# The tail of a row-skewness kernel: one partial sum moved from VectorE to ScalarE, VectorE's last two steps made one

## Chip, cores and metric

One core of one Trainium2 chip. The metric is device time in microseconds (us) of one execution; a number for a kernel is the median of its runs. Engine names are those of the profile: PE (TensorE matmul), PEld (TensorE weight load), DVE (VectorE), ACT (ScalarE), POOL (GpSimd), SP (SyncE). A trailing q (DVEq, ACTq, SPq) is the engine's sequencer, which handles waits and issues.

## What is computed

```python
rows, cols = 1024, 8192          # x: float32
mean = np.mean(x, axis=-1, keepdims=True)
std = np.std(x, axis=-1, keepdims=True)
z = (x - mean) / (std + 1e-8)
return np.mean(z ** 3, axis=-1)
```

The kernel computes it from raw moments. With m1, m2, m3 the row means of x, x² and x³, and var = m2 − m1², the skewness is (m3 − 3·m1·(m2 − (2/3)·m1²)) · var^(−1.5).

## The kernel before

**Blocks.** The 1024 rows are 8 blocks of 128 rows (row p·8+b is partition p of block b). A block is loaded in units (`UNITS`, line 19): two of 4096 columns in the first four blocks, and ever smaller ones behind that, the last block in eight units of 1152, 1152, 1152, 896, 1024, 1152, 896 and 768 columns. All loads are issued on SP's queue (line 206) into eight rotating buffers. The order of work on each engine is the order in the source (a manual schedule); waits between instructions are added by the framework.

**Per slice.** ScalarE squares a slice of x and accumulates its sum into one column of `s2u` (line 213, an ACTIVATE and an accumulator read). VectorE multiplies the square by x and accumulates into one column of `s3u` (line 218, a SCALAR_TENSOR_TENSOR and an accumulator read). TensorE transposes x in chunks of 128 columns and adds the transposes up in PSUM (line 231). In the last block one slice is one unit, so its eight slices fill eight columns of `s2u` and `s3u`; the square of the very last slice goes to PSUM (`sqps`) and not to SBUF.

**Statistics.** The blocks 0 to 6 are finished while the last block is worked on (lines 146 to 197). The tail of the last block (lines 241 to 263) is what the change touches:

- ScalarE copies the transposed sums out of PSUM (line 127) and sums the eight columns of `s2u` into `m2` and the first six of `s3u` into `m3` (line 247). The last two columns of `s3u`, those of the last but one slice (`j - 2`) and of the last one (`j - 1`), are not ready yet.
- TensorE turns the copy into the row means `m1` (line 130).
- ScalarE makes `m1sq` = m1² (line 253), `nm1` = −3·m1 (line 254), `v3` = m2 − (2/3)·m1sq (line 255) and `t` = nm1·v3 + m3 (line 256).
- GpSimd makes `var` = m2 − m1sq (line 257) and `rr` = var^(−1.5) (line 258).
- VectorE, behind its last slice (`cube`, line 218), makes `num` = s3u[j−2] + t + s3u[j−1] (line 259), then `skew` = num·rr (line 263).
- SP waits for the last eight loads (lines 265 to 267) and for VectorE's last step, and writes the result out (line 268).

The profile shortens names: `m_l` may be `m2` or `m3` of the tail, `v_l` is `v3`, `nm_l` is `nm1`.

**Waits.** In the built program a compute instruction holds one semaphore wait itself; further ones go to a wait instruction on the same engine's sequencer just ahead of it (the DVEq, ACTq rows of the trace). `num` has a sequencer wait for VectorE's own last accumulator read and holds a wait for `t` itself. `skew` has a sequencer wait for `num` and holds a wait for `rr` itself. `v3` holds a wait for `m1sq`, and `t` one for `v3`, both of their own engine.

Of the kernel before, what the change touches and what calls it, by code (L numbers as in the profile page):

```python
# [9 lines left out]
AF = mybir.ActivationFunctionType  # L10
ALU = mybir.AluOpType
# [48 lines left out]
def kernel(  # L60
# [11 lines left out]
    NB = R // P  # L72
    L = NB - 1
# [22 lines left out]
    def small(name, n):  # L96
        return onep.tile([P, n], FP, tag=name, name=name)
# [9 lines left out]
    s2u, s3u = sums[:, 0 : NB * K], sums[:, NB * K :]  # L107
# [5 lines left out]
    skew = small("skew", NB)  # L113
# [4 lines left out]
    act, g, v = nc.scalar.activation, nc.gpsimd, nc.vector  # L118
# [10 lines left out]
    def mean(b):  # L129
        nc.tensor.matmul(  # L130
            out=s1ps[:, b : b + 1], lhsT=Tsb[b % 2], rhs=onesn, start=True, stop=True
        )
# [23 lines left out]
    def first_rest():  # L156
# [8 lines left out]
        out=m1a[:, 0:nw], in0=s1ps[:, 0:nw], in1=s1a, op=ALU.add))  # L165
# [23 lines left out]
    def third_2():  # L189
# [7 lines left out]
        out=skew[:, F : F + 1], in0=mid["t"], in1=mid["rr"], op=ALU.mult))  # L197

    for b, widths in enumerate(UNITS):
        tp = tps[b] = psum.tile([P, P], FP, tag="tp", name=f"tp_{b}")  # L200
        c0 = 0
        j = b * K
        for k, (w, n_slices) in enumerate(widths):
# [4 lines left out]
            for s, e in _slices(w, n_slices):  # L208
                if last_unit:
                    sq = psum1.tile([P, e - s], FP, tag="sqps", name="sqps")  # L210
                else:
                    sq = sqpool.tile([P, e - s], FP, tag="sq", name=f"sq_{b}_{k}_{s}")
                act(  # L213
                    out=sq, in_=xt[:, s:e], func=AF.Square, scale=s_scale,
# [4 lines left out]
                    out=cube, in0=sq, scalar=1.0, in1=xt[:, s:e],  # L219
                    op0=ALU.mult, op1=ALU.mult, accum_out=s3u[:, j : j + 1],  # L220
# [3 lines left out]
            if w_act:  # L224
                act(  # L225
                    out=same[:, 0:w_act], in_=xt[:, w - w_act : w], func=AF.Copy,
                    scale=inv_n, accum_out=s1a[:, b : b + 1],
                )
            n = (w - w_act) // P
            for c in range(n):  # L230
                nc.tensor.matmul(  # L231
                    out=tp, lhsT=xt[:, c * P : (c + 1) * P], rhs=ident,
# [6 lines left out]


    n, m1 = n_sl[L], s1ps[:, L : L + 1]
    m2, m3, m1sq, nm1, var, v3, rr, t, num = (
        small(f"{t}_l", 1) for t in ("m2", "m3", "m1sq", "nm1", "var", "v3", "rr", "t", "num")
    )

    def row_sum(out, src, n):
        act(out=junk[:, 0:n], in_=src[:, L * K : L * K + n], func=AF.Copy, accum_out=out)

    copy_sums(L)
    row_sum(m2, s2u, n)  # L250
    row_sum(m3, s3u, n - 2)
    mean(L)
    act(out=m1sq, in_=m1, func=AF.Square)
    act(out=nm1, in_=m1, func=AF.Copy, scale=-3.0)
    act(out=v3, in_=m1sq, func=AF.Identity, scale=-2.0 / 3.0, bias=m2)
    act(out=t, in_=v3, func=AF.Identity, scale=nm1, bias=m3)
    g.tensor_tensor(out=var, in0=m2, in1=m1sq, op=ALU.subtract)
    g.tensor_tensor(out=rr, in0=var, in1=expo[:, 0:1], op=ALU.pow)
    v.scalar_tensor_tensor(  # L259
        out=num, in0=s3u[:, j - 2 : j - 1], scalar=t, in1=s3u[:, j - 1 : j],  # L260
        op0=ALU.add, op1=ALU.add,
    )
    v.tensor_tensor(out=skew[:, L:NB], in0=num, in1=rr, op=ALU.mult)  # L263

    seen = nc.sync.nop()
    for ld in loads[-8:]:
# [32 lines left out]
```

## Time and profile before

| | |
|---|---|
| median of 5 runs | 90.92 us (90.86 to 91.01) |
| the profiled execution: time | 90.89 us |
| its span, first to last instruction | 89.1 us |
| time outside of the span | 1.79 us |
| granted TensorE clock, mean | 0.97 |
| DVE, ACT busy | 74.1 us (83%), 74.2 us (83%) |
| VectorE's last slice ends | 86.25 us into the span |
| the last compute step (`skew`) ends | 86.85 us into the span |
| write of the result: issue, issue to landing | at 86.88 us, 1.4 us |

The time is the whole execution, the span what lies between its first and last instruction. A timeline row reads: start in us from the span's beginning, length in us, engine, source line, operation, output<-inputs, shape; what stands in square brackets is how long the engine was idle and what released it. "issue" in the chain of work is time in which an engine waited for nothing that the profile shows.

### The profile page before, as it was taken

The page shows a single profiled execution, that of the slowest core. Times are in us where ns is not written, and L with a number is a line of the kernel's source. Part 1 is how long each engine was busy: PE and PEld are TensorE (multiplying, and loading weights), DVE is VectorE, ACT ScalarE, POOL GpSimd, SP SyncE. Part 2 cuts the span into 40 slices and gives each one's busy share as a digit, 9 for nine tenths or more (in the row PEclk, how much of TensorE's full clock was granted, in tenths as well). Part 3 has the DMA queues.
Part 4 walks back from the last instruction along what each step waited for, and adds up shares of the span by engine and source line. Part 5 has one row for each costly group of instructions (what it writes and reads, how often), then busy time and mean ns, then how long its engine had stood idle before and what let it go on. Part 6 is the DMA issues. An engine that isn't in the chain of part 4 may idle for free.

```text
span 89.1 us, 1436 instructions
## 1 busy us (share of the span) xinstructions
PE 63.5 (71%) x504; PEld 58.2 (65%) x504; DVE 74.1 (83%) x111; ACT 74.2 (83%) x136; POOL 13.7 (15%) x18
## 2 busy tenths in 40 slices
PE   0002999583492935999998899488997989888910
PEld 0002989482491925999997799378896868677710
DVE  1000399999799498999999999999999999999980
ACT  6002999789992999999799999599999999999960
POOL 3000000000000000000000000000000089999830
PEclk9999999999999999569999999999999999999995
DMA  4899999999999999999999999999999999997000
GB/s 118 324 419 441 434 419 441 434 419 441 434 419 427 427 427 427 434 419 433 408 436 394 413 436 422 430 419 419 419 403 430 405 412 414 407 409 273 17 0 2
DMA packets 4038, 33.64 MB, mean 378 GB/s; under 512 B 576, under 2 KB 576, under 8 KB 2368
## 3 DMA queue, kind: packets, MB, share of 16 engines
q1 hardware_dynamic: 4032, 33.56, 90.5%
q8 instruction: 4, 0.07, 0.3%
q14 instruction: 2, 0.02, 0.0%
HBM read 33.55 MB, written 0.00 MB: 377 GB/s over the span
## 4 chain that ended last, share of the span: by engine, by line
DMA 55%; DVE 22%; issue 10%; ACT 5%; SPq 4%; DVEq 0%; ACTq 0%
DMA x<-in_x_dram 55%; DVE sq L218 21%; ACT sq L213 5%; SPq L206 4%; DVE cube L218 1%; DVE num_l L259 0%; DVE skew L263 0%; DVE m23m L176 0%; DVEq L218 0%; DVEq L263 0%; DVEq L259 0%; ACTq L213 0%
## 5 line engine op out<-in xcount | busy, mean ns | idle before, releaser
L218 DVE SCALAR_TENSOR_TENSOR sq<-sq,x 128x1568 f32<-128x1568 f32 (+20 forms) x51 | 72.3, 1477 | 11.7 <-ACT sq L213 11.5
L213 ACT ACTIVATE sq<-x 128x1568 f32<-128x1568 f32 (+20 forms) x51 | 63.9, 1256 | 11.2 <-DMA x<-in_x_dram 10.7
L231 PE MATMUL tp<-ident,x 128*128 128x128 f32 x488 | 61.5, 285 | 14.4 <-DMA x<-in_x_dram 14.2
L231 PEld LDWEIGHTS tp<-ident,x 128*128 128x128 f32 x488 | 56.8, 148 | 17.9 <-DMA x<-in_x_dram 9.2
L153 POOL TENSOR_TENSOR vara<-m23a,m1sqa 128x6 f32<-128x6 f32 x1 | 2.0, 1987 | 70.4 <-ACT m1sq3a L157 70.4
L213 ACT ACTIVATION_READ_ACCUMULATOR sq<-x 128x1 f32 x51 | 9.5, 186 | 0.0
L130 PEld LDWEIGHTS s1ps<-onesn,tsb 128*128 128x128 f32 x16 | 2.4, 188 | 9.1 <-ACT tsb L127 9.1
L130 PE MATMUL s1ps<-onesn,tsb 128*128 128x1 f32 x16 | 3.0, 254 | 7.4 <-ACT tsb L127 7.4
L218 DVE DVE_READ_ACCUMULATOR sq<-sq,x 128x1 f32 x51 | 4.2, 82 | 0.0
L225 ACT ACTIVATE same<-x 128x1024 f32<-128x1024 f32 x3 | 3.1, 1041 | 0.0
L154 POOL TENSOR_TENSOR rra<-vara,expo 128x6 f32<-128x6 f32 x1 | 2.9, 2877 | 0.1
L127 ACT COPY tsb<-tp 128x128 f32<-128x128 f32 x8 | 1.9, 244 | 0.0
L102 ACT ACT_TABLE_LOAD x1 | 1.3, 1283 | 0.7 <-PEq L283 0.7
L184 POOL TENSOR_TENSOR rr<-var,expo 128x1 f32<-128x1 f32 x1 | 1.4, 1427 | 0.1
L161 POOL TENSOR_TENSOR m23a<-m23a,m1sq3a 128x6 f32<-128x6 f32 x1 | 1.3, 1268 | 0.1
L160 POOL TENSOR_TENSOR m1sq3a<-m1sq3a,nm1a 128x6 f32<-128x6 f32 x1 | 1.2, 1202 | 0.1
L162 POOL TENSOR_TENSOR skew<-m23a,rra 128x6 f32<-128x6 f32 x1 | 1.2, 1201 | 0.1
L183 POOL TENSOR_TENSOR var<-m23m,m1sq 128x1 f32<-128x1 f32 x1 | 1.0, 1043 | 0.0
L218 DVE SCALAR_TENSOR_TENSOR cube<-sqps,x 128x768 f32<-128x768 f32 x1 | 1.0, 955 | 0.0
L196 POOL TENSOR_TENSOR skew<-t,rr 128x1 f32<-128x1 f32 x1 | 0.8, 842 | 0.1
L213 ACT ACTIVATE sqps<-x 128x768 f32<-128x768 f32 x1 | 0.8, 796 | 0.0
L100 DVE MEMSET onesn<- 128x1 f32 x1 | 0.1, 59 | 0.8 <-PEq L283 0.8
(34 smaller groups left out, 7.8 us busy)
## 6 DMA issues: line engine op xcount, KB each, us to landing
x<-in_x_dram SPq DMA_DIRECT2D x8, 2048.0 KB, 23.6
x<-in_x_dram SPq DMA_DIRECT2D x2, 1472.0 KB, 30.0
x<-in_x_dram SPq DMA_DIRECT2D x3, 832.0 KB, 18.0
x<-in_x_dram SPq DMA_DIRECT2D x4, 576.0 KB, 10.7
x<-in_x_dram SPq DMA_DIRECT2D x2, 896.0 KB, 22.9
x<-in_x_dram SPq DMA_DIRECT2D x1, 1728.0 KB, 32.8
x<-in_x_dram SPq DMA_DIRECT2D x1, 1408.0 KB, 25.3
x<-in_x_dram SPq DMA_DIRECT2D x1, 1216.0 KB, 23.4
```

Of the source, the lines that this page charges most:

```text
L102: nc.scalar.activation(out=tiny, in_=onesn, func=AF.Square)
L127: nc.scalar.copy(out=Tsb[b % 2], in_=tps[b])
L130: nc.tensor.matmul(out=s1ps[:, b : b + 1], lhsT=Tsb[b % 2], rhs=onesn, start=True, stop=True)
L153: g.tensor_tensor(out=vara, in0=m2a, in1=m1sqa, op=ALU.subtract)
L154: g.tensor_tensor(out=rra, in0=vara, in1=expo, op=ALU.pow)
L161: g.tensor_tensor(out=m3a, in0=m3a, in1=m1sq3a, op=ALU.add)
L184: g.tensor_tensor(out=mid["rr"], in0=mid["var"], in1=expo[:, 0:1], op=ALU.pow)
L206: loads.append(nc.sync.dma_start(out=xt, in_=xv[b, :, c0 : c0 + w]))
L213: act(out=sq, in_=xt[:, s:e], func=AF.Square, scale=s_scale, accum_out=s2u[:, j : j + 1],)
L218: v.scalar_tensor_tensor(out=cube, in0=sq, scalar=1.0, in1=xt[:, s:e], op0=ALU.mult, op1=ALU.mult, accum_out=s3u[:, j : j + 1],)
L225: act(out=same[:, 0:w_act], in_=xt[:, w - w_act : w], func=AF.Copy, scale=inv_n, accum_out=s1a[:, b : b + 1],)
L231: nc.tensor.matmul(out=tp, lhsT=xt[:, c * P : (c + 1) * P], rhs=ident, start=(k == 0 and c == 0), stop=(c0 == C and c == n - 1), is_transp ...
```

## The change

ScalarE's sum of the first six columns of `s3u` goes to a tile of its own, `m3p`. A new ScalarE instruction, between `nm1` and `v3`, adds the column of the last but one slice to it: `m3` = s3u[j−2] + m3p. `t` now holds seven of the eight columns, and VectorE's two closing steps become one: skew = (s3u[j−1] + t)·rr. The tile `num` goes.

```diff
-    m2, m3, m1sq, nm1, var, v3, rr, t, num = (
-        small(f"{t}_l", 1) for t in ("m2", "m3", "m1sq", "nm1", "var", "v3", "rr", "t", "num")
+    m2, m3p, m3, m1sq, nm1, var, v3, rr, t = (
+        small(f"{t}_l", 1) for t in ("m2", "m3p", "m3", "m1sq", "nm1", "var", "v3", "rr", "t")
     )
...
     copy_sums(L)
     row_sum(m2, s2u, n)
-    row_sum(m3, s3u, n - 2)
+    row_sum(m3p, s3u, n - 2)
     mean(L)
     act(out=m1sq, in_=m1, func=AF.Square)
     act(out=nm1, in_=m1, func=AF.Copy, scale=-3.0)
+    act(out=m3, in_=s3u[:, j - 2 : j - 1], func=AF.Identity, bias=m3p)
     act(out=v3, in_=m1sq, func=AF.Identity, scale=-2.0 / 3.0, bias=m2)
     act(out=t, in_=v3, func=AF.Identity, scale=nm1, bias=m3)
     g.tensor_tensor(out=var, in0=m2, in1=m1sq, op=ALU.subtract)
     g.tensor_tensor(out=rr, in0=var, in1=expo[:, 0:1], op=ALU.pow)
     v.scalar_tensor_tensor(
-        out=num, in0=s3u[:, j - 2 : j - 1], scalar=t, in1=s3u[:, j - 1 : j],
-        op0=ALU.add, op1=ALU.add,
+        out=skew[:, L:NB], in0=s3u[:, j - 1 : j], scalar=t, in1=rr,
+        op0=ALU.add, op1=ALU.mult,
     )
-    v.tensor_tensor(out=skew[:, L:NB], in0=num, in1=rr, op=ALU.mult)
```

In the built program the new ScalarE instruction has a sequencer wait for VectorE's accumulator read of the last but one slice, and holds a wait for `m3p`. VectorE's closing step has one sequencer wait for two things, its own last accumulator read and `t`, and holds a wait for `rr`. On PE nothing differs. On GpSimd the same instructions stand in the same order with the same waits. SP issues the same transfers in the same order; the write of the result waits for VectorE's closing step as before.

## The prediction

> **What bounds the kernel now.** I read the page's first part and its chain of work first, then the chain in order of time from 84 us on, then the timelines of ScalarE and GpSimd over the same stretch. On the page:
>
> ```profile
> span 89.1 us, 1436 instructions
> ...
> DMA 55%; DVE 22%; issue 10%; ACT 5%; SPq 4%; DVEq 0%; ACTq 0%
> ```
>
> The chain is loading for over half of the span and VectorE's slices after that. The change touches nothing of either: its first edited instruction runs after 85 us, so only the last 1.5 us before the write can move. That stretch of the chain (start us, length us, what):
>
> ```profile
> 84.27 1.10 DVE sq L218 x3
> 85.37 0.89 DVE cube L218 x2
> 86.26 0.03 issue
> 86.29 0.02 DVEq L259
> 86.31 0.06 issue
> 86.37 0.23 DVE num_l L259
> 86.60 0.03 issue
> 86.62 0.02 DVEq L263
> 86.64 0.04 issue
> 86.69 0.16 DVE skew L263
> ```
>
> VectorE's last slice with its accumulator read ends at 86.26. Then 0.11 us go by for a sequencer wait and the start (0.03 + 0.02 + 0.06), num takes 0.23, another 0.09 go by in the same way, and skew takes 0.16 to 86.85. SP issues the write at 86.88. All behind that (the write's 1.4 us and the program's end) waits for this one instant, so the time moves one for one with the end of VectorE's closing step: 86.85 before.
>
> What ScalarE does meanwhile, from its timeline; the first three rows are the same operation in the block before, with the instructions around it:
>
> ```profile
> 79.90 0.18 ACT L213 ACTIVATION_READ_ACCUMULATOR sq<-x 128x1 f32 x1
> 79.99 0.28 ACT L187 ACTIVATE v<-m1sq,m23m 128x1 f32<-128x1 f32 x1
> 80.20 1.06 ACT L213 ACTIVATE sq<-x 128x1024 f32<-128x1024 f32 x1
> ...
> 85.34 0.17 ACT L253 ACTIVATE m1sq_l<-s1ps 128x1 f32<-128x1 f32 x1
> 85.41 0.17 ACT L254 ACTIVATE nm_l<-s1ps 128x1 f32<-128x1 f32 x1
> 85.54 0.29 ACT L255 ACTIVATE v_l<-m1sq_l,m_l 128x1 f32<-128x1 f32 x1
> 85.87 0.39 ACT L256 ACTIVATE t_l<-v_l,m_l,nm_l 128x1 f32<-128x1 f32 x1
> ```
>
> t ends at 86.26, in the same instant as VectorE's last slice: the two arms are level, with nothing to spare that could be counted on. Two rules of ScalarE are to be read here. Instructions with no wait on each other overlap: nm_l starts 0.07 after m1sq_l starts. Instructions that wait on each other don't: v_l starts 0.03 after m1sq_l ends (85.51), t_l 0.04 after v_l ends (85.83). The third arm is GpSimd's:
>
> ```profile
> 85.59 0.19 POOL L257 TENSOR_TENSOR var_l<-m_l,m1sq_l 128x1 f32<-128x1 f32 x1 [1.19 <-ACT nm_l L254]
> 85.86 0.54 POOL L258 TENSOR_TENSOR rr_l<-var_l,expo 128x1 f32<-128x1 f32 x1
> ```
>
> rr ends at 86.40 by this rough record. Before, only skew at 86.69 needed it; now the closing step does, at once.
>
> **What goes from VectorE.** Before, 86.26 to 86.85 is 0.11 + 0.23 + 0.09 + 0.16 = 0.59 us. After, one wait and one step: 0.11 and 0.22 (the duration of num, 218 ns, which has the same operation, shape and a pointer scalar as the new step). With all its inputs ready the closing step would run 86.37 to 86.59, 0.26 us earlier. That is the most that the change can give: 90.92 − 0.26 = **90.66 us**.
>
> **What comes to ScalarE.** The new m3 is an ACTIVATE with one pointer operand (its bias) on 128x1, as L187 is; that row gives 0.28 us, and the next instruction on ScalarE started 0.21 after it (79.99 to 80.20), its wait over by then or not, so 0.21 is what m3 holds the engine for at the most in that row. Its start: nm_l ends at 85.58, and back-to-back rows overlap by about 0.09 (79.90 + 0.18 against 79.99), so the engine has room from 85.49. m3 adds a wait, for VectorE's accumulator read of the last but one slice, which ends at 85.37; with the 0.11 of a sequencer wait and start that is 85.48, level with the engine's own 85.49. So this wait costs about nothing, and if VectorE is later in some execution its own last slice is later by the same, before and after. Queued behind m3 are v3 and t, and for t waits VectorE's closing step. I take m3 from 85.50.
>
> - v3 starts at 85.50 + 0.21 = 85.71 instead of 85.54 (m1sq has long ended) and ends 0.29 later at 86.00.
> - t starts 0.04 after that, at 86.04, and ends 0.39 later at 86.43 instead of 86.26.
> - The sequencer wait on VectorE, now for its own slice and for t together, ends with t: 86.43 + 0.11 = 86.54. Closing step to 86.54 + 0.22 = **86.76**.
>
> m2, m1sq and nm1 stand ahead of m3, so GpSimd's var and rr start as before. SP's queue is moved past nothing, and its transfers are the same.
>
> **What rr may cost.** No row of before shows VectorE held up by GpSimd. From below: rr ends at 86.40, and an engine holding its wait itself starts 0.04 after the release in the rows of ScalarE to VectorE (accumulator read 30.23 + 0.18, VectorE from 30.45): 86.44, earlier than 86.54, so nothing. From above: skew, which held the same wait, ran at 86.69, so rr was there by then, and the closing step would end at 86.69 + 0.22 = 86.91. I take the lower end, since the record of rr's end is the nearest row and it would have to be off by 0.10 to count.
>
> **Sum.** 86.76 − 86.85 = −0.09 us. Against the profiled execution that is 90.89 − 0.09 = 90.80; that execution lies 0.03 below the median of the runs, so for a median I forecast 90.92 − 0.09 = **90.83 us**. Of 0.26 us that leave VectorE, 0.17 come back as a later t.
>
> **A rule of the skill against it.** The trace has VectorE's plain add at 0.16 us (skew, TENSOR_TENSOR) and its add with a pointer at 0.22, and ScalarE's at 0.28. The Trainium skill, "ScalarE: Activation LUTs", section "Rules for kernel authors", would keep an add on VectorE. By that rule alone, with each add priced as a lone instruction, the move would lose 0.28 − 0.16 = 0.12 us. The rows agree on the prices, but the rule is about work per element, and here each step on VectorE also has 0.09 to 0.11 of wait and start. The same page, section "What ACT_TABLE_LOAD costs", gives an overlap of about 93 ns between back-to-back ACTIVATEs and about 280 ns for one with a pointer bias; by those, as an estimate, m3 would hold the engine 0.19 us and t would end 0.02 earlier.
>
> **Rivals.** About 0.2% (0.18 us) is what a measurement of this kernel can tell from no change, so the lines are at 90.74 and 91.10.
>
> 1. *ScalarE hides most of m3.* m1sq and nm1 start 0.07 apart. If m3 too gives its place up after 0.07, t ends at 86.33, the closing step starts at 86.44 (where rr also lets it) and ends at 86.66: −0.19, **90.73 us**, with 90.66 as the floor. For it: ScalarE idles in v3's wait for m1sq before (85.49 to 85.54), and the 0.21 behind L187 may hold some of the next load's wait. Against: those two take immediate operands and last 0.17; L187 with a pointer lasts 0.28.
> 2. *rr becomes the bound.* GpSimd's records are rough. If rr is seen only between 86.54 and 86.69, the time lies between 90.83 and 90.92 + 0.06 = **90.98 us**. For it: nothing before shows that rr was early. Against: two records, 0.19 and 0.54 long, would have to be short by some tenth.
> 3. *ScalarE doesn't overlap at m3, and the change loses.* If m3 with its sequencer wait starts only when nm1 has ended, and v3 only when m3 has ended, m3 runs from 85.58 + 0.11 = 85.69 to 85.97, v3 from 86.01 to 86.30, t from 86.34 to 86.73, and the closing step from 86.84 to 87.06: +0.21, **91.13 us**. Without the 0.11 at m3's start (0.03 in its place) it is 0.08 less, 91.05. The place is the ScalarE stretch from nm1 to t. It decides from the point where t comes over 0.26 us later than before (86.52); beyond 86.70 the loss is over 0.2%. For it: t has two fresh inputs and v3 and t are already strictly serial. Against: v3 doesn't use m3, and L187, which also has a sequencer wait, started 0.09 before the instruction ahead of it ended.
>
> That the change does not do what it says is excluded by the built order: one instruction less on VectorE, one more on ScalarE, in the places given.
>
> **Chances and range.** Forecast 0.60, rival 1 0.20, rival 2 0.10, rival 3 0.10. Faster by over 0.2%: rival 1 with 0.20, and 0.05 of the forecast, whose 0.09 a scatter such as that of the five runs (0.15 between the ends) can carry over the line: 0.25. Slower by over 0.2%: 0.08 of rival 3. Within: 0.55 + 0.10 + 0.02 = 0.67. The range goes from the floor, 90.66, to rival 3 with the short start, 91.05, which takes in both ends of rr; only rival 3's far end, under 1 in 10, is left out.
>
> **What would show it.** In the changed profile: an ACTIVATE m3 at about 85.50, 0.28 long; v3 about 0.21 after its start; t ending at 86.43, clearly behind VectorE's last slice at 86.26; one closing step of 0.22, started 0.11 after t's end; the distance from the end of VectorE's last slice to the end of the closing step 0.50 instead of 0.59. If v3 starts 0.07 behind m3, it is rival 1; if the step starts well over 0.11 after t, it is rival 2; if v3 starts only after m3's end, rival 3. A change anywhere ahead of 85 us would make the working wrong as a whole.

## The result and the profile after

| | before | after |
|---|---|---|
| median | 90.96 us (90.83 to 91.30, 47 runs) | 90.84 us (90.66 to 91.04, 26 runs) |
| ratio after / before | | 0.9984, 95% interval 0.9978 to 0.9991 |
| profiled execution: time, span | 90.89, 89.1 us | 90.72, 88.9 us |
| end of VectorE's last accumulator read | 86.25 us | 86.23 us |
| end of the closing step | 86.85 us | 86.67 us |
| **tail**: from the one to the other | 0.60 us | 0.44 us |

The ratio is a gain of 0.15 us (0.08 to 0.20), under the 0.2% line of the prediction. The first column holds 47 runs where the table ahead of the prediction has 5, and its median is 0.04 us higher. All comparisons below are ratios to runs of before on the same chip. Where they are too coarse, the tail is read from a kernel's one profile; two further profiles show how far to trust it: late_before has the tail of before (0.60) and late_after that of after (0.44), each within 0.01 us. The expectations give after's tail as 0.43; by the rows it is 86.67 − 86.23 = 0.44.

The page after counts one compute instruction less on VectorE (110 for 111) and one more on ScalarE (137 for 136); the one by which the total falls is a wait of SP behind the write. The chain no longer ends on VectorE's slices but runs through ScalarE:

```profile
span 88.9 us, 1435 instructions
...
DMA 62%; ACT 23%; issue 5%; SPq 4%; DVE 2%; ACTq 0%; DVEq 0%
```

The larger share of ACT does not come from more work there (74.4 us busy, 74.2 before): VectorE and ScalarE run side by side for most of the span, and the chain, followed back from the end, now passes along ScalarE. Its last pieces in order of time (start us, length us, what):

```profile
85.40 0.05 issue
85.45 0.29 ACT m_l L255
85.74 0.19 ACT v_l L256
85.94 0.02 issue
85.96 0.40 ACT t_l L257
86.36 0.04 DVEq L260
86.39 0.06 issue
86.45 0.22 DVE skew L260
```

VectorE's sequencer wait ends with t at 86.36 + 0.04, and the closing step starts 0.06 later: by this chain t decides. The timeline of the same stretch after, ScalarE and GpSimd, then VectorE's last two rows:

```profile
85.32 0.17 ACT L253 ACTIVATE m1sq_l<-s1ps 128x1 f32<-128x1 f32 x1
85.39 0.17 ACT L254 ACTIVATE nm_l<-s1ps 128x1 f32<-128x1 f32 x1
85.45 0.29 ACT L255 ACTIVATE m_l<-sums,m3p_l 128x1 f32<-128x1 f32 x1
85.56 0.19 POOL L258 TENSOR_TENSOR var_l<-m_l,m1sq_l 128x1 f32<-128x1 f32 x1 [1.18 <-ACT nm_l L254]
85.65 0.28 ACT L256 ACTIVATE v_l<-m1sq_l,m_l 128x1 f32<-128x1 f32 x1
85.83 0.54 POOL L259 TENSOR_TENSOR rr_l<-var_l,expo 128x1 f32<-128x1 f32 x1
85.96 0.39 ACT L257 ACTIVATE t_l<-v_l,m_l,nm_l 128x1 f32<-128x1 f32 x1
86.15 0.08 DVE L218 DVE_READ_ACCUMULATOR cube<-sqps,x 128x1 f32 x1
86.45 0.22 DVE L260 SCALAR_TENSOR_TENSOR skew<-sums,t_l,rr_l 128x1 f32<-128x1 f32 x1 [0.22 <-POOL rr_l L259]
```

m3 (`m_l`, L255) starts 0.06 behind nm1, v3 starts 0.20 behind m3 while m3 is still running (to 85.74), and t ends at 86.35. Before, t ended 0.01 behind VectorE's slice; now it ends 0.12 behind it. So the added instruction made t 0.11 later, not 0.17. rr ends at 86.37, as far behind VectorE's slice (0.14) as before within 0.02. Which of the two, t or rr, the closing step waits for can't be told from ends that lie 0.02 apart: the chain goes through t, the last row names rr. That is what the first experiments are for. Theory A is that t decides and that m3 made it late; theory B is that rr decides and t has slack.

### The profile page after: what moved, and what is told of

The parts are those of the page before. It is cut to its first block, busy times and chain, and to the rows that moved or that the text cites. A ratio compares the mean times of both kernels' runs of the same rounds, so it can differ in the third digit from the quotient of the medians.

```text
span 88.9 us, 1435 instructions
## 1 busy us (share of the span) xinstructions
PE 63.5 (71%) x504; PEld 58.3 (66%) x504; DVE 73.9 (83%) x110; ACT 74.4 (84%) x137; POOL 13.6 (15%) x18
## 4 chain that ended last, share of the span: by engine, by line
DMA 62%; ACT 23%; issue 5%; SPq 4%; DVE 2%; ACTq 0%; DVEq 0%
DMA x<-in_x_dram 62%; ACT sq L213 19%; SPq L206 4%; DVE sq L218 2%; ACT sqps L213 1%; ACT junk L247 1%; ACT t_l L257 0%; ACT m_l L255 0%; ACT t L190 0%; DVE skew L260 0%; ACT v_l L256 0%; ACT v L187 0%; ACT tsb L127 0%; ACT m1sq3a L157 0%; ACT nm1a L158 0%
```

## The experiments

All tails are from the end of VectorE's last accumulator read to the end of the closing step.

### 1. The added half alone: two_steps

Edit of the changed kernel:

```diff
-        out=skew[:, L:NB], in0=s3u[:, j - 1 : j], scalar=t, in1=rr,
-        op0=ALU.add, op1=ALU.mult,
+        out=num, in0=s3u[:, j - 1 : j], scalar=t, in1=sums[:, K - 1 : K],
+        op0=ALU.add, op1=ALU.add,
     )
+    v.tensor_tensor(out=skew[:, L:NB], in0=num, in1=rr, op=ALU.mult)
```

> The added half of the change alone: ScalarE adds the last but one column (m3), and VectorE still ends with two steps with a wait between them, num = s3u[j-1] + t + a column of zeros, then skew = num x rr. The result is the same. Tail = time from the end of VectorE's last accumulator read to the end of the closing step, 0.60 us before and 0.43 us after the change. Theory A (t is the arm that decides after the change, m3 made it 0.11 later against VectorE's last slice): num starts 0.10 behind t's end, tail = 0.22 + 0.22 + 0.10 + 0.16 = 0.70, so slower than before by 0.10 us (ratio 1.001). Theory B (GpSimd's rr decides after the change, t has slack): rr is only needed by skew, which is late anyway, num starts behind VectorE's own slice as before, tail 0.60, the time of before.

Measured: ratio 0.9999 (0.9990 to 1.0009), the time of before. In the profile VectorE's last read ends at 86.24, and t ends as late behind it as in the changed kernel (0.12); the chain's last pieces:

```profile
85.97 0.40 ACT t_l L257
86.36 0.02 issue
86.39 0.23 DVE num_l L261
...
86.71 0.16 DVE skew L265
```

The tail is 0.63. The chain runs through t, as theory A has it, but num starts only 0.03 behind t, not 0.10. Here num holds the wait for t itself, and the sequencer wait ahead of it (for VectorE's own slice) is over by then. Where the late one sits in the sequencer wait, as in the changed kernel, it costs 0.10. So the added instruction alone costs 0.03 in the tail and not 0.10: a miss in size that came from the price of the wait. The times are too coarse to show 0.03.

### 2. The fused step alone: no_m3

Edit of the changed kernel:

```diff
-    act(out=m3, in_=s3u[:, j - 2 : j - 1], func=AF.Identity, bias=m3p)
...
-    act(out=t, in_=v3, func=AF.Identity, scale=nm1, bias=m3)
+    act(out=t, in_=v3, func=AF.Identity, scale=nm1, bias=m3p)
```

> The fused closing step alone: ScalarE does not add the last but one column, which is left out of the sum altogether. So ScalarE's tail is that of before, VectorE's that of after. Theory A (t decides after the change): t ends level with VectorE's slice again, the closing step starts at whichever comes later, 0.11 behind the slice or some 0.04 to 0.08 behind rr (0.14 behind the slice in the changed profile): tail 0.33 to 0.44; by A alone 0.36, some 0.24 us faster than before, 0.07 faster than after. Theory B (rr decides, 0.08 behind its end): tail stays 0.43 to 0.44, as after, 0.17 us faster than before.

Measured: ratio 0.9966 (0.9954 to 0.9978), 0.31 us faster than before (0.20 to 0.42), with after's interval not reaching that ratio. The profiled execution is the slowest of the twelve (90.98; their median is 90.71). In it VectorE ran 0.23 us later than in before's profile, and it did so long before the edited lines (the slice at 78.51 us stood 0.23 later too), while ScalarE stood as in it (m1sq starts at 85.33, 85.34 before), so t (86.26) and rr (86.39) were ready before VectorE's last slice ended. Its chain is VectorE's alone:

```profile
85.59 0.89 DVE cube L218 x2
86.48 0.03 issue
86.51 0.05 DVEq L259
86.56 0.06 issue
86.62 0.22 DVE skew L259
```

The tail is 0.37: VectorE's last read ends at 86.47, and 0.15 later, behind the waits and the start (0.03 + 0.05 + 0.06 in the chain), the step of 0.22 begins. The sequencer wait for two things took 0.05 and not the 0.02 of before. That is the floor of the fused step, 0.23 under before's 0.60. So the removal is worth up to 0.23, and the changed kernel keeps 0.16 of it: 0.07 of its tail come from t. The times say more than the tail here (0.31 against 0.23); the interval takes 0.23 in, and what the rest is stays open. That profile can't tell what rr would do with VectorE on time; run 6 gives the price for it. It also shows VectorE elsewhere against ScalarE than the other profiles have it, which run 8 takes up.

### 3. The power taken out of the closing step: no_rr

Edit of the changed kernel:

```diff
-        out=skew[:, L:NB], in0=s3u[:, j - 1 : j], scalar=t, in1=rr,
+        out=skew[:, L:NB], in0=s3u[:, j - 1 : j], scalar=t, in1=mid["rr"],
```

> The changed kernel, but its closing step multiplies by the power of the block before (long ready), so it does not wait for the last block's rr, which is still computed; the last block's power is left out of the result. The number and places of the waits are the same. Theory A (t decides): tail 0.43, the time of after. Theory B (rr decides): the tail is shorter than 0.43, by as much as rr is later than t; as both ended within 0.02 us in the changed profile, by 0.02 to 0.05 at the most, since the wait for t comes next.

Measured: tail 0.44 (VectorE's last read ends at 86.18; t ends at 86.30):

```profile
85.91 0.39 ACT L257 ACTIVATE t_l<-v_l,m_l,nm_l 128x1 f32<-128x1 f32 x1
...
86.40 0.22 DVE L260 SCALAR_TENSOR_TENSOR skew<-sums,t_l,rr 128x1 f32<-128x1 f32 x1 [0.22 <-POOL rr_l L259]
86.77 0.35 SPq L268 DMA_DIRECT2D out_dram<-skew  x1
```

The step starts 0.10 behind t, as in after, though it doesn't read the last block's rr: theory A. The releaser that the row names, rr_l, isn't read by this step at all: releasers are inferred, and between two ends so close the inference picked the wrong one. The time, ratio 0.9989 (0.9978 to 1.0000), is not to be set against after: the third row shows the write issued 0.15 behind the closing step where after has 0.03 (86.70 behind 86.67). The instructions in the trace explain it: the write now holds a wait for GpSimd itself, and the wait for VectorE moved into a wait instruction on SP's sequencer, with a second one behind it.

### 4. The disputed instruction twice: m3_twice

Edit of the changed kernel:

```diff
     act(out=m3, in_=s3u[:, j - 2 : j - 1], func=AF.Identity, bias=m3p)
+    act(out=spare, in_=sums[:, K - 1 : K], func=AF.Identity, bias=m3p)
```

> The changed kernel with a second such ACTIVATE (128x1, pointer bias, on a column of zeros, result unused) right behind m3 and ahead of v3. Doubles the cost in dispute. Theory A with m3 priced by its place in the queue (0.20 us from its start to v3's): v3 starts 0.40 behind m3's start, t ends 0.20 later, tail 0.63 to 0.64, 0.20 us slower than after and 0.03 slower than before. If ScalarE hid most of such an instruction (a place of 0.07): tail 0.50. If each held the engine for its whole length (0.28): tail 0.71. Theory B (rr decides, t has slack): less than 0.20 by that slack, which the changed profile puts under 0.02.

Measured: ratio 0.9999 (0.9987 to 1.0012), 0.14 us over after's ratio, though the intervals overlap at their ends (after's reaches 0.9991). The profile is sharper; ScalarE's rows:

```profile
85.39 0.29 ACT L255 ACTIVATE m_l<-sums,m3p_l 128x1 f32<-128x1 f32 x1
85.59 0.28 ACT L257 ACTIVATE spare_l<-sums,m3p_l 128x1 f32<-128x1 f32 x1
85.77 0.28 ACT L258 ACTIVATE v_l<-m1sq_l,m_l 128x1 f32<-128x1 f32 x1
86.08 0.39 ACT L259 ACTIVATE t_l<-v_l,m_l,nm_l 128x1 f32<-128x1 f32 x1
```

Starts lie 0.20 and 0.18 apart: that is the place such an instruction takes. t ends 0.31 behind VectorE's last read (86.16), where after has 0.12, and the tail is 0.63, 0.19 more. That is theory A with its price, to 0.01 us. ScalarE neither hides it (a place of 0.07) nor runs it strictly alone (0.28).

### 5. Is it the new wait? m3_no_wait, and the order: m3_behind_v3

m3_no_wait, edit of the changed kernel:

```diff
-    row_sum(m3p, s3u, n - 2)
+    row_sum(m3p, s3u, n - 3)
...
-    act(out=m3, in_=s3u[:, j - 2 : j - 1], func=AF.Identity, bias=m3p)
+    act(out=m3, in_=s3u[:, j - 3 : j - 2], func=AF.Identity, bias=m3p)
```

> The changed kernel, but m3 adds the column ahead of it (s3u[j-3], ready 1 us earlier; the accumulating sum takes one column less), so that the column of the last but one slice is left out. The new wait for VectorE is still there but long over. Theory A1 (the new wait costs nothing, m3's start is set by ScalarE's own issue 0.06 behind nm1): m3 starts 0.06 behind nm1, tail 0.43, the time of after. Theory A2 (the wait for VectorE's accumulator read, which ended 0.10 ahead of m3's start in the changed profile, sets it): m3 starts earlier, by the 0.02 to 0.03 that ScalarE would allow, tail 0.40 to 0.41.

Measured: ratio 0.9983 (0.9975 to 0.9992), tail 0.42, m3 0.05 behind nm1 (85.57 and 85.62). That is after within 0.02 in the tail and 0.01 in m3's start, nearer to A1 than to A2: with VectorE on time, the new wait costs 0.01 at most. It is no more than level, though: in after it is over at 85.40, 0.05 ahead of m3's start, and in late_after, where it does decide, 0.05 ahead as well.

m3_behind_v3, edit of the changed kernel:

```diff
-    act(out=m3, in_=s3u[:, j - 2 : j - 1], func=AF.Identity, bias=m3p)
     act(out=v3, in_=m1sq, func=AF.Identity, scale=-2.0 / 3.0, bias=m2)
+    act(out=m3, in_=s3u[:, j - 2 : j - 1], func=AF.Identity, bias=m3p)
```

> The changed kernel with m3 and v3 in the other order; same result. v3 starts at once behind m1sq (0.03 behind its end, 0.20 behind m1sq's start), m3 takes its place behind it (0.20), t waits for m3. Theory A (t decides, place of 0.20): m3 starts 0.40 behind m1sq's start and ends 0.68 behind it, t starts 0.71 behind it instead of 0.64, tail 0.50, 0.07 us slower than after. If m3 hid behind v3 (ScalarE takes it up 0.07 later): t starts 0.56 behind m1sq, then rr or the slice decide, tail 0.36 to 0.44.

Measured: ratio 0.9991 (0.9981 to 1.0001). In the profile t starts 0.72 behind m1sq, where after has 0.64, and the tail is 0.52, 0.08 over after:

```profile
85.66 0.17 ACT L253 ACTIVATE m1sq_l<-s1ps 128x1 f32<-128x1 f32 x1
...
85.86 0.29 ACT L255 ACTIVATE v_l<-m1sq_l,m_l 128x1 f32<-128x1 f32 x1
86.06 0.28 ACT L256 ACTIVATE m_l<-sums,m3p_l 128x1 f32<-128x1 f32 x1
86.38 0.39 ACT L257 ACTIVATE t_l<-v_l,m_l,nm_l 128x1 f32<-128x1 f32 x1
```

This is what theory A expects. m3 ahead of v3 is the better place, since it starts in the 0.06 that v3 would spend waiting for m1sq.

### 6. The addition on GpSimd: m3_pool

Edit of the changed kernel:

```diff
-    act(out=m3, in_=s3u[:, j - 2 : j - 1], func=AF.Identity, bias=m3p)
+    g.tensor_tensor(out=m3, in0=m3p, in1=s3u[:, j - 2 : j - 1], op=ALU.add)
```

> The changed kernel with the new addition on GpSimd, ahead of var, instead of on ScalarE; same result. t is early again; rr is later. GpSimd waits for VectorE's read of the last but one slice, so by the records (0.19 a step, 0.08 between steps) m3 takes the place in which var stood or one just ahead of it, and var and rr come 0.13 to 0.19 later. If rr then decides (theory B's price for GpSimd: 0.08 from its end to the closing step): tail 0.56 to 0.63, 0.13 to 0.20 us slower than after, about the time of before. If GpSimd's records are too long and rr has slack of 0.2 or more: tail 0.36, faster than after by 0.07.

Measured: ratio 0.9985 (0.9975 to 0.9994); the times don't tell it from after. t ends early, at 86.33, 0.06 behind VectorE's last read; now GpSimd decides:

```profile
85.54 0.19 POOL L255 TENSOR_TENSOR m_l<-m3p_l,sums 128x1 f32<-128x1 f32 x1 [1.12 <-ACT m1sq_l L253]
85.69 0.19 POOL L258 TENSOR_TENSOR var_l<-m_l,m1sq_l 128x1 f32<-128x1 f32 x1
85.95 0.55 POOL L259 TENSOR_TENSOR rr_l<-var_l,expo 128x1 f32<-128x1 f32 x1
86.19 0.08 DVE L218 DVE_READ_ACCUMULATOR cube<-sqps,x 128x1 f32 x1
86.54 0.22 DVE L260 SCALAR_TENSOR_TENSOR skew<-sums,t_l,rr_l 128x1 f32<-128x1 f32 x1 [0.26 <-POOL rr_l L259]
```

The tail is 0.48, between the two expected cases: rr decides, but m3 and var don't wait for each other and overlap, so it came only 0.09 later against VectorE. The closing step started 0.04 behind rr. With that price, rr in the changed kernel would have let the step start at 86.37 + 0.04 = 86.41; it started at 86.45. So rr is the second arm there, with 0.04 to spare. By the same price, as an estimate, a kernel without m3 that does need rr would start its step at rr's end, 0.14 to 0.15 behind VectorE's slice, plus 0.04, for a tail of 0.40 to 0.41: with VectorE on time the floor of run 2 could not be reached, and m3 costs the changed kernel only 0.03 to 0.04 over that.

### 7. Neither arm: no_m3_no_rr

Edit of the changed kernel:

```diff
-    act(out=m3, in_=s3u[:, j - 2 : j - 1], func=AF.Identity, bias=m3p)
...
-        out=skew[:, L:NB], in0=s3u[:, j - 1 : j], scalar=t, in1=rr,
+        out=skew[:, L:NB], in0=s3u[:, j - 1 : j], scalar=t, in1=mid["rr"],
```

(and t reads m3p, as in no_m3.)

> The fused closing step with neither of the two arms: the last but one column is left out of the sum (no m3), and the step multiplies by the power of the block before. Only VectorE's own last slice, and a t that ends level with it, are left. All theories: the floor, tail 0.36 (0.03 for the release, 0.05 for the sequencer's wait, 0.06 to the start, 0.22 for the step). With VectorE level with ScalarE as in the profile before, the step may start 0.10 behind t instead: tail 0.36 to 0.37. If the same number comes here as without m3 alone (0.9966 in the earlier run), rr costs nothing once m3 is gone; if this is faster than that by 0.05 or more, rr had decided there in most executions.

Measured: tail 0.37, the floor of run 2, now with VectorE on time. The step starts at 86.54, 0.15 behind VectorE's read (86.30 + 0.09) and t (86.39):

```profile
86.30 0.09 DVE L218 DVE_READ_ACCUMULATOR cube<-sqps,x 128x1 f32 x1
86.54 0.22 DVE L259 SCALAR_TENSOR_TENSOR skew<-sums,t_l,rr 128x1 f32<-128x1 f32 x1
```

The time, ratio 0.9993 (0.9980 to 1.0007), carries the same extra 0.12 us on SP as run 3 (write issued at 86.91, the step ended at 86.76), so the comparison of times that the expectation wanted can't be drawn; only the tail can be compared.

### 8. VectorE made late, in both kernels: late_before and late_after

The same edit of both kernels:

```diff
+    idle = small("idle", P)
+    at(L, 5, lambda: v.tensor_tensor(out=idle, in0=ident, in1=ident, op=ALU.add))
```

> The kernel before with one idle step put on VectorE ahead of its last but one slice (adds two constant 128x128 tiles, result unused; about 0.25 us of its queue by the length of a 128x1 step, 0.16, and 1 element per 0.96 GHz clock as its longer steps show: 1.02 us for 896 columns against 0.89 for 768). So VectorE's last slice ends 0.25 later against ScalarE, and t and rr are ready well ahead. All theories: tail 0.60 as before, since VectorE's own chain set it there; the time is 0.25 us above that of before (ratio 1.0027).

> The changed kernel with the same idle step on VectorE. The prediction's step said that if VectorE is later the new wait makes m3 later by the same, so the gain stays (tail 0.43, time 0.17 under late_before). Theory C (t has a chain of 0.90 us from m1sq on, and only m3 starts from VectorE's read, so part of t's lateness is covered when VectorE is late): m3 starts 0.10 behind the read of the last but one slice; that read ends 0.89 ahead of the end of VectorE's last one; v3 0.20 later, t 0.32 behind that, 0.39 long: t ends 1.01 behind that read, so 0.12 behind VectorE's end, as in the changed profile, if m3 waits for the read; tail 0.43 to 0.44. If ScalarE's v3 has been ready and the wait is shorter than 0.10, tail 0.37 to 0.43. So: 0.43 speaks for the prediction's step, 0.37 against it.

Measured: late_before 1.0022 (1.0011 to 1.0034), late_after 1.0011 (0.9993 to 1.0029), 91.19 and 91.02 us: 0.17 apart by the medians, 0.10 by the ratios, and the intervals overlap. VectorE's last two slices stand 0.20 later against ScalarE in both profiles. The tails are 0.60 and 0.44, as without the idle step. The chain of late_after:

```profile
85.72 0.02 ACTq L258
85.73 0.04 issue
85.78 0.29 ACT m_l L258
86.07 0.20 ACT v_l L259
86.27 0.03 issue
86.29 0.39 ACT t_l L260
86.69 0.04 DVEq L263
86.72 0.06 issue
86.78 0.22 DVE skew L263
```

nm1 started at 85.51 here, so m3 was free to start at 85.57; it started at 85.78, 0.09 behind VectorE's read of the last but one slice (85.60 + 0.09 = 85.69). The new wait (`ACTq`) is what sets m3 now, and t's arm moves with VectorE, for the same tail. The prediction's step holds, and the shorter tail that theory C allowed did not come. So when VectorE is late the change gains no more than when it is on time: t can't use the slack. The same trace settles t against rr a second time:

```profile
85.96 0.54 POOL L262 TENSOR_TENSOR rr_l<-var_l,expo 128x1 f32<-128x1 f32 x1
```

rr ends at 86.50 here, ahead of VectorE's last read (86.57) and 0.28 ahead of the closing step, and still the step starts 0.10 behind t and the tail is that of after. In after the step starts at the same distance behind t, so there too it was t.

## Why the prediction was right, point by point

- **The bound and the place.** Right. In the profiled pair the closing step ends 0.18 earlier; 0.02 of it is VectorE's last slice, and the other 0.16 lie in the tail.
- **What goes from VectorE, 0.26 us.** Its mechanism is shown by run 2, and its size was a little high: 0.23. The fused step's sequencer waits for two things, VectorE's own read and t, and took 0.05 where the sum used the 0.02 of a wait for one. As estimated in run 6, rr would have kept some 0.03 more of it.
- **What m3 costs t, 0.17 us.** This is the term that was mis-sized: 0.11 in the profile. m3 started 0.06 behind nm1 instead of 0.09, held its place for 0.20 instead of 0.21, and t followed v3's start by 0.31 instead of 0.33. Those three make the 0.06 by which the tail came out under the 0.50 of the forecast (0.44). Place and mechanism are shown by doubling it (0.18 to 0.20 a place) and by moving it (0.08 more).
- **The new wait, nothing.** Right to 0.01 with VectorE on time (run 5), and right that the gain stays with VectorE late (run 8), where the wait does set m3's start.
- **rr, nothing.** Right: without it the tail is the same (run 3), and with rr early it is the same too (run 8). The margin is 0.04 (run 6), smaller than the 0.10 of the prediction, since t came earlier.
- **The sum.** −0.09 forecast, −0.16 in the profiles' tails, −0.15 (−0.20 to −0.08) in the times. The forecast lies at the weak end of the interval. The truth stood between the forecast and rival 1, nearer to rival 1 in size, though not by its mechanism: ScalarE does not hide m3 after 0.07. That the median came out within 0.01 of 90.83 is partly luck, as before's own median was 0.04 higher in more runs.
- **Rivals 2 and 3.** Rival 2 (rr) was 0.04 us away. Rival 3 (no overlap on ScalarE) is excluded by v3's start at 85.65, ahead of m3's end at 85.74.
- **The Trainium skill's rule against it** ("ScalarE: Activation LUTs", "Rules for kernel authors": an add belongs on VectorE). Read as the price of a lone instruction it gave a loss of 0.12 us. On VectorE the step that left cost its 0.16 and a wait and start of 0.09, and of the 0.20 that the one that came takes in ScalarE's queue, 0.11 showed in t and 0.07 in the tail over its floor: the measurement decides for the move. The same page's overlap of about 93 ns ("What ACT_TABLE_LOAD costs") fits m3's place: 0.29 long, 0.20 from start to start.

## What to carry to other kernels

This is one kernel; what follows is read from its tail. In a tail of 128x1 steps, count for each engine the places in its queue and the hand-overs, not the durations: a dependent step on the engine that ends the chain costs its length and 0.09 to 0.11 us, an independent one on an engine with a gap costs its place (0.20 here) less the gap. When two arms end level, taking work from one makes the other the bound, so the worth of a removal (0.23 here) is to be cut by what the other arm then lacks (0.07 here) before it is believed. Where a step waits for several things, look at which wait it holds itself and which goes to the sequencer: the one that comes last is best the one held. That last advice is read from the starts listed below; no run moved a wait and left all else as it was.

## What the runs showed of the hardware

- A wait that the late instruction holds itself costs 0.03 us from the release to the start (two_steps, t to num) or 0.04 (m3_pool, rr to the closing step); a release of t through a sequencer wait costs 0.10 (after, no_rr, m3_twice, m3_no_wait, m3_behind_v3 and late_after, t to the closing step). Behind its own last read VectorE started 0.12 later through a sequencer wait for that one thing (before) and 0.15 later through one for two things (no_m3, no_m3_no_rr).
- VectorE's place against ScalarE can move by more than the effect that was measured: in one of the ten profiles without the idle step (no_m3) it stood 0.23 us later, with ScalarE's tail in the same place; the other nine agree within 0.02. Why is open. Runs of one kernel spread over 0.4 us (after: 90.66 to 91.04), so the tail in a profile said more than a handful of times.
- An engine's wait can be put down to the wrong releaser where two ends lie within 0.05 us: no_rr's closing step was shown as waiting for a tile that it doesn't read.
